# Two 16 KB activation tiles are placed ahead of the small constants in the on-chip memory, in a three-layer fp32 network on one core

## The chip, the cores and the metric

The kernel runs on 1 core of one Trainium2 chip. The metric is device time of one execution in microseconds (us), the median of several runs; lower is better. In names below, PE is TensorE, DVE is VectorE, ACT is ScalarE, POOL is GpSimd, SP is SyncE; PEld are the weight loads of PE. SBUF is the on-chip memory of 128 partitions in which all tiles lie; a tile's address is a byte within each partition.

## The reference

Three layers act on one sequence of 512 positions with 1024 features, all in float32. Cut to what matters:

```python
def hybrid_layer(x, ...):                      # twice
    u = rms_norm(x, g_mix_pre) @ w_in          # 1024 -> 3200
    aq, ak, av, cu, rq, rk, rv, rg = split(u)
    mix = concat([chunk_attention(aq, ak, av), conv_module(cu), retention(rq, rk, rv, rg)]) @ w_out
    x = x + rms_norm(mix, g_mix_post)
    f = square(relu(rms_norm(x, g_mlp_pre) @ w_up)) @ w_down      # 1024 -> 4096 -> 1024
    return x + rms_norm(f, g_mlp_post)

def second_block(x, ...):                      # once
    q, k, v, u, gates = split(rmsnorm(h, norm1_gain) @ w_in)      # 1024 -> 5632
    branches: difference attention on q, k, v; a state-space layer on u; sigmoid(gates)
    h = h + (g_attn * attn_branch + g_ssm * ssm_branch) @ w_out
    up = causal_dwconv(rmsnorm(h, norm2_gain) @ w_up)             # 1024 -> 5632
    gate, val = split(up)
    return h + (silu(gate) * val) @ w_down                        # 2816 -> 1024
```

## The kernel before

**Three matmuls for one.** Float32 products are made from the type float32r, in which one matmul pass does not keep all bits. Each operand is therefore split into a high part (a cast) and a low part (the rest), and each 128x128 block product takes three matmuls: high by high, high by low, low by high (`mm3`, L863, and `t_part`, L911). PE is given a stationary operand (128 columns, loaded beforehand) and a moving operand (up to 512 columns, streamed).

```python
nc.tensor.matmul(ps, whi, ahi, start=start, stop=False)     # out, stationary, moving
nc.tensor.matmul(ps, whi, alo, start=False, stop=False)
nc.tensor.matmul(ps, wlo, ahi, start=False, stop=stop)
```

**The tiles of the change.** `hhi` and `hlo` (L999, L1000) hold the high and low part of the normalised activations, transposed: 128 partitions of 8 x 512 floats, 16,384 bytes of a partition each. `to_hT` (L985) writes them, before each of the large products that start from the normalised x. They are read in two ways:

- In `f_unit` (L890) and `f_split` (L896) a chunk of weights (tiles `whi`, `wlo`) is stationary and `hhi`/`hlo` move, 512 columns at a time (256 in `f_split`). So are made w_up of all layers, most of the first layers' w_in, the gates, and the attention projection, for which the two tiles are filled anew. The same function, with other moving tiles (`ghi`, `glo`, `shi`, `slo`), makes w_glu and w_ssm_proj.
- In `t_unit` (L922) 128 columns of `hhi`/`hlo` are stationary and the weights move, 384 or 512 columns at a time: v, q and k of the layers. The same function makes w_down and w_out, with `fhi`/`flo`, `mixhi`/`mixlo` or `mhi`/`mlo` stationary.

A trace names a matmul `ps<-moving,stationary`, so `ps<-hhi,whi` is of the first kind and `ps<-whi,hhi` of the second.

**The rest of the work.** Weights stream from HBM through SP's queue in chunks of 128x1024 floats into 4 slots (`wraw`); ACT casts each into `whi`, DVE or POOL subtracts to make `wlo` (4 slots each). Attention, retention, convolution and the state-space layer run as side tasks on DVE, ACT and POOL between the matmuls.

**The order of the work.** The program is recorded first (`Builder.run`), then a planner (`Trace.order`, L443) sets the order of all instructions by its own costs and due times, and `issue` (L638) writes them out in that order. The planner looks at which slot of a pool a tile has, never at an address.

**Where a tile lies.** Tiles are lazy: the real one is made when the first instruction that uses it is written out (L324, L365). `hhi`, `hlo` and the constants come from the pool `cp` (`bufs` None), which gives each new tile the next free bytes, rounded up to 32.

```python
    def place(self):
        if self.real is None:
            self.real = self.pool.make(self)
        return self.real
```

So the order of first use sets the addresses. Before, this is `mhalf` (128 bytes, from byte 16512), `ones` (512), `epsc` (4), `cm` (2048), `pv` (3208), `hhi`, `rope` (1024), `hlo`, and some small ones. `hhi` starts at byte 22464 and `hlo` at byte 39872; both are 192 bytes past a multiple of 256. The slots of `wraw`, `whi` and `wlo` (from byte 61184, 4096 each) and the 55 slots of the pool `sp` (from byte 110336, 2048 each), in which every other large tile lies, start at multiples of 256. Any block of `hhi` or `hlo` that a matmul reads starts a multiple of 512 bytes into the tile.

Of the kernel before, what the change touches and what calls it, by code (L numbers as in the profile page):

```python
# [2060 lines left out]
@with_exitstack  # L2061
def hybrid_stack_kernel(ctx: ExitStack, tc, A, out):
    b = Builder(tc, ctx, A, out)
    b.run()
    order = b.nc.order()
    with tc.manual_schedule():
        b.nc.issue(order)

# [17 lines left out]
```

## Time and profile before

| what | value |
|---|---|
| median of 3 runs | 2149.17 us (2148.69 to 2149.26) |
| the profiled execution: its own time | 2147.38 us |
| its span, first to last instruction | 2145.7 us |
| PE busy | 2050.4 us, 96% of the span, 9964 matmuls |
| DVE / ACT / POOL busy | 64% / 43% / 34% |
| DMA | 105 GB/s mean |

A matmul's recorded length is longer than the distance to the next one, since matmuls overlap in the pipeline. This distance, from start to start, is called the pitch here. It is read from a timeline (starts of two matmuls, divided by the steps between them) or from a window in which PE never stops: in a window of 20 us with 90 matmuls, the first one began up to its own length of 0.39 us earlier, so the pitch is about (20 + 0.39) / 90 = 226.6 ns.

A row of the view by windows has, in this order: the window's start and end, its length, the busy time (and number of instructions) of PE, PEld, DVE, ACT and, where it worked, POOL, the granted share of PE's clock, the DMA engines' busy share and the GB/s they moved.

### The profile page before, as it was taken

How to read it: one execution, taken by the hardware profiler on the slowest of the kernel's cores; microseconds unless marked ns; L12 is line 12 of the kernel's file. 1: busy time of each engine (PE TensorE's matmuls, PEld its weight loads, DVE VectorE, ACT ScalarE, POOL GpSimd, SP SyncE). 2: the span in 40 equal slices, each digit the busy share in tenths (PEclk: the TensorE clock that was granted, in tenths of full speed). 3: DMA queues.
4: the chain of work that ended last, by engine and by line, in shares of the span. 5: the costliest groups of instructions: out<-in, count | busy, mean ns of one | idle time of the engine just before them, and what ended most of it. 6: DMA issues, size and time to landing. Idle time of an engine off the chain costs nothing. (4 is left out here: it accounts for less than half of the span.)

```text
span 2145.7 us, 27037 instructions
## 1 busy us (share of the span) xinstructions
PE 2050.4 (96%) x9964; PEld 1703.7 (79%) x9964; DVE 1365.4 (64%) x2127; ACT 931.5 (43%) x1527; POOL 726.4 (34%) x858
## 2 busy tenths in 40 slices
PE   7998989999999998899999999999999999999999
PEld 7987778778889977688888887677777788888887
DVE  5998795344458998553454473478889546655545
ACT  3377534222334376443233244456578234333322
POOL 3662367960005652300000036754653431000000
PEclk9999999999999999999999998999999999999999
DMA  5423333333243332223233363222324423233322
GB/s 180 128 61 126 109 104 128 109 108 98 79 125 96 121 96 92 95 83 99 79 105 102 89 205 117 90 84 74 97 75 157 157 79 109 89 99 98 99 79 79
DMA packets 85556, 225.16 MB, mean 105 GB/s; under 512 B 10416, under 2 KB 20400, under 8 KB 85424
## 3 DMA queue, kind: packets, MB, share of 16 engines
q1 hardware_dynamic: 85424, 223.43, 32.7%
q8 instruction: 79, 1.29, 0.3%
q14 instruction: 53, 0.43, 0.1%
HBM read 204.25 MB, written 19.14 MB: 104 GB/s over the span
## 5 line engine op out<-in xcount | busy, mean ns | idle before, releaser
L642 POOL TENSOR_TENSOR wlo<-wraw,whi 128x1024 fp32r<-128x1024 f32 (+1 forms) x156 | 365.8, 2353 | 1079.5 <-ACT whi L642 883.3
L642 ACT CAST whi<-wraw 128x1024 fp32r<-128x1024 f32 (+1 forms) x323 | 330.4, 1029 | 703.8 <-PE ps L642 567.2
L642 PE MATMUL ps<-hhi,whi 128*128 128x512 f32 (+1 forms) x1488 | 506.8, 370 | 7.5 <-DVE acc L642 1.9
L642 PE MATMUL ps<-hlo,whi 128*128 128x512 f32 (+1 forms) x1488 | 505.8, 369 | 6.9 <-DVE hlo L642 6.9
L642 PE MATMUL ps<-hhi,wlo 128*128 128x512 f32 (+1 forms) x1488 | 505.3, 369 | 0.5 <-DVE wlo L642 0.5
L642 PEld LDWEIGHTS ps<-hhi,whi 128*128 128x128 f32 x1488 | 273.0, 191 | 56.3 <-issue 4.1
L642 PEld LDWEIGHTS ps<-hlo,whi 128*128 128x128 f32 x1488 | 272.8, 191 | 54.6 <-DVE hlo L642 7.9
L642 PEld LDWEIGHTS ps<-hhi,wlo 128*128 128x128 f32 x1488 | 272.3, 191 | 48.9 <-DVE wlo L642 1.4
L642 DVE TENSOR_TENSOR wlo<-wraw,whi 128x1024 fp32r<-128x1024 f32 x178 | 223.9, 1259 | 114.7 <-ACT whi L642 114.2
L642 PE MATMUL ps<-whi,fhi 128*128 128x512 f32 x688 | 249.6, 392 | 4.8 <-DVE t L642 2.4
L642 PE MATMUL ps<-whi,flo 128*128 128x512 f32 x688 | 249.8, 391 | 0.0
L642 PE MATMUL ps<-wlo,fhi 128*128 128x512 f32 x688 | 249.7, 391 | 0.0
L642 DVE TENSOR_TENSOR acc<-ps,acc 128x512 f32<-128x512 f32 x112 | 76.5, 687 | 155.1 <-PE ps L642 155.1
L642 PE MATMUL ps<-wlo,hhi 128*128 128x384 f32 (+1 forms) x448 | 157.5, 371 | 3.9 <-POOL wlo L642 3.9
L642 PE MATMUL ps<-whi,hhi 128*128 128x384 f32 (+1 forms) x448 | 156.0, 372 | 0.9 <-ACT whi L642 0.7
L642 PEld LDWEIGHTS ps<-whi,fhi 128*128 128x128 f32 x688 | 129.5, 188 | 33.3 <-DVE t L642 2.9
L642 PE MATMUL ps<-whi,hlo 128*128 128x384 f32 (+1 forms) x448 | 155.2, 369 | 0.0
L642 PEld LDWEIGHTS ps<-whi,flo 128*128 128x128 f32 x688 | 129.7, 188 | 28.0
L642 PEld LDWEIGHTS ps<-wlo,fhi 128*128 128x128 f32 x688 | 129.7, 189 | 27.8
L642 POOL TENSOR_TENSOR st<-st,mhalf 128x1 f32<-128x1 f32 (+1 forms) x56 | 55.0, 983 | 194.9 <-DVE st L642 192.9
L642 DVE TENSOR_SCALAR t<-ps 128x512 f32<-128x512 f32 x64 | 44.1, 690 | 93.9 <-PE ps L642 93.8
L642 DVE TENSOR_TENSOR X<-ps,X 128x512 f32<-128x512 f32 x56 | 38.6, 689 | 92.3 <-PE ps L642 92.1
(249 smaller groups left out, 3250.2 us busy)
## 6 DMA issues: line engine op xcount, KB each, us to landing
wraw<-in_wst SPq DMA_DIRECT2D x302, 512.0 KB, 3.5
wraw<-in_wst SPq DMA_DIRECT2D x32, 384.0 KB, 3.1
gain<-in_gains SPq DMA_DIRECT2D x20, 256.0 KB, 4.3
X<-in_x SPq DMA_DIRECT2D x16, 256.0 KB, 5.4
xd<-X SPq DMA_DIRECT2D x16, 256.0 KB, 2.1
X<-xd SPq DMA_DIRECT2D x16, 256.0 KB, 5.6
gated<-t SPq DMA_DIRECT2D x16, 256.0 KB, 2.1
gate<-gated SPq DMA_DIRECT2D x16, 256.0 KB, 3.7
```

Source lines behind the costliest of these rows:

```text
L642: getattr(getattr(self.nc, e), m)(*[r(x) for x in op.args], **{k: r(v) for k, v in op.kw.items()})
```

## The change

Right after the planner has set the order, three tiles are made, before the first instruction is written out: `mhalf`, then `hhi` and `hlo`.

```diff
     b.run()
     order = b.nc.order()
+    for t in (b.mhalf, b.hhi, b.hlo):
+        t.place()
     with tc.manual_schedule():
         b.nc.issue(order)
```

`mhalf` is named first because it is 128 bytes long and the pool begins 128 bytes past a multiple of 256. `hhi` now starts at byte 16640 and `hlo` at byte 33024, both multiples of 256. `ones`, `epsc`, `cm`, `pv` and `rope` follow at 49408 to 56256 and keep their distance to the last multiple of 256 (0, 0, 32, 32 and 192 bytes). Every other tile keeps its address. No instruction is added, removed or changed but for these addresses, and on each of the five engines the instructions stand in the same order, row for row.

## Rows read from the trace of the kernel before

**Rows 1.** The page's head: span, and busy time by engine.

```profile
span 2145.7 us, 27037 instructions
PE 2050.4 (96%) x9964; PEld 1703.7 (79%) x9964; DVE 1365.4 (64%) x2127; ACT 931.5 (43%) x1527; POOL 726.4 (34%) x858
```

**Rows 2.** The chain of work that ended last: start, length, what.

```profile
1780.76 361.13 PE ps L642 x1640
```

**Rows 3.** Groups of PE's instructions by form: count, busy us, mean ns of one.

```profile
L642 PE MATMUL ps<-hhi,wlo 128*128 128x512 f32 x1104 | 420.1, 397 | 0.5 <-DVE wlo L642 0.5
L642 PE MATMUL ps<-whi,flo 128*128 128x512 f32 x688 | 249.8, 391 | 0.0
L642 PE MATMUL ps<-whi,hlo 128*128 128x384 f32 x256 | 79.1, 338 | 0.0
L642 PE MATMUL ps<-wlo,hhi 128*128 128x512 f32 x192 | 78.1, 413 | 0.0
L642 PE MATMUL ps<-klo,stk 128*128 128x512 f32 x40 | 16.4, 409 | 3.9 <-DVE klo L642 3.9
```

**Rows 4.** Windows without a stop: two of hhi/hlo moving, two of weights moving.

```profile
1800.00:1864.00 64.00, 64.00 (x276) 51.58 (x275) 39.23 (x48) 27.19 (x36) 2.40 (x1) 1.00 0.31 99
1687.00:1727.00 40.00, 40.00 (x173) 32.20 (x173) 29.37 (x21) 11.54 (x14) 18.70 (x8) 1.00 0.46 158
1739.00:1759.00 20.00, 20.00 (x90) 16.49 (x89) 2.77 (x4) 6.55 (x11) 9.47 (x4) 1.00 0.37 103
2118.00:2135.00 17.00, 17.00 (x77) 14.08 (x76) 7.88 (x10) 2.11 (x2) 0.00 (x0) 1.00 0.04 16
```

**Rows 5.** Timeline of PE where f_unit has shi and slo moving: start, length.

```profile
1666.23 0.50 PE L642 MATMUL ps<-slo,whi 128*128 128x512 f32 x1 [0.97 <-DVE slo L642]
...
1667.72 0.40 PE L642 MATMUL ps<-shi,whi 128*128 128x512 f32 x1
...
1669.10 0.62 PE L642 MATMUL ps<-shi,whi 128*128 128x512 f32 x2
...
1671.82 0.39 PE L642 MATMUL ps<-shi,whi 128*128 128x512 f32 x1
```

**Rows 6.** Timeline of PE with hhi and hlo stationary, weights moving.

```profile
84.04 0.34 PE L642 MATMUL ps<-whi,hhi 128*128 128x384 f32 x1
...
85.60 0.34 PE L642 MATMUL ps<-whi,hhi 128*128 128x384 f32 x1
...
1583.67 0.40 PE L642 MATMUL ps<-whi,hlo 128*128 128x512 f32 x1
...
1586.94 0.40 PE L642 MATMUL ps<-whi,hhi 128*128 128x512 f32 x1
```

**Rows 7.** Timeline of PE in f_split, 256 columns of hhi and hlo moving.

```profile
1774.69 0.28 PE L642 MATMUL ps<-hhi,whi 128*128 128x256 f32 x1
...
1775.03 0.28 PE L642 MATMUL ps<-hhi,whi 128*128 128x256 f32 x1
```

**Rows 8.** Windows, stretches where PE hardly stops.

```profile
500.00:600.00 100.00, 100.00 (x436) 81.53 (x435) 48.30 (x54) 31.74 (x39) 8.07 (x3) 1.00 0.36 106
350.00:450.00 100.00, 92.36 (x381) 73.27 (x380) 40.36 (x61) 27.49 (x34) 97.34 (x259) 0.96 0.35 116
935.00:1265.00 330.00, 330.00 (x1444) 269.68 (x1443) 156.15 (x194) 108.08 (x146) 18.89 (x12) 1.00 0.33 102
1680.00:1730.00 50.00, 50.00 (x217) 40.44 (x216) 32.94 (x24) 13.74 (x16) 21.41 (x10) 1.00 0.45 152
1798.00:2141.00 343.00, 343.00 (x1488) 279.04 (x1487) 188.96 (x229) 114.99 (x145) 12.06 (x5) 1.00 0.29 91
```

**Rows 9.** Windows, the stretches with side tasks.

```profile
0.00:300.00 300.00, 266.69 (x1509) 237.58 (x1510) 248.53 (x441) 159.87 (x301) 146.89 (x160) 0.98 0.35 114
650.00:935.00 285.00, 262.44 (x1512) 234.05 (x1511) 233.16 (x378) 151.86 (x290) 123.15 (x138) 0.99 0.30 96
1265.00:1680.00 415.00, 388.85 (x1923) 306.63 (x1922) 296.45 (x539) 244.49 (x440) 230.30 (x169) 0.98 0.35 110
```

## The prediction

> **What bounds the kernel now.** I read the page's head first [rows 1]: PE is busy 2050.4 of 2145.7 us, so only about 95 us of the span are not matmuls. The chain of waits says the same of the end: its last piece but one is 361 us of PE without a wait, 1640 matmuls one behind the other [rows 2]. So the time is, for the most part, the number of matmuls times their pitch, and the question is whether an address can change a pitch.
>
> The groups by form then show something odd [rows 3]. With 512 columns moving, `ps<-hhi,wlo` lasts 397 ns on average and `ps<-whi,flo` 391 ns. These means hold waits and a slower clock in places, so I went to windows without a stop, all at a granted clock of 1.00 [rows 4]. Where `hhi`/`hlo` move, 276 matmuls fill 64 us: (64 + 0.40) / 276 = **233.3 ns** each; the second such window gives (40 + 0.40) / 173 = 233.5. Where weights move and `mhi`/`mlo` are stationary, (20 + 0.39) / 90 = **226.6 ns**; the window near the end, with `fhi`/`flo`, gives 225.8. The shape and the type are the same in all four. Other engines hardly matter: the fourth window, with POOL idle, is as fast as the third, with POOL at work half of the time, and the first is slow with POOL as good as idle.
>
> The two kinds differ in who moves, so a control is needed. Rows 5 are it: the same function `f_unit`, weights stationary, but `shi`/`slo` moving, which lie in slots of `sp` at multiples of 256. From 1669.10 to 1671.82 there are 12 steps: 2.72 / 12 = 226.7 ns. So not the function and not the roles make 233; what is left is the tile, and the programmed difference of `hhi` and `hlo` is their start, 192 bytes past a multiple of 256. As stationary operand they seem to cost as well: from 1583.67 to 1586.94 are 14 steps of 233.6 ns with 512 columns of weights moving, and from 84.04 to 85.60 nine steps of 173.3 ns with 384 columns [rows 6]; three quarters of 226.7 would be 170.0.
>
> **The change part by part.** No instruction is added, removed or reordered, so no queue is passed and no wait is new. `ones`, `epsc`, `cm`, `pv` and `rope` move, but keep their distance to a multiple of 256: I cost them at nothing, between no gain and no loss. ACT's and DVE's writes of the two tiles I cost at nothing too: they lie beside PE's work in all but a few places. What can change is the pitch of every matmul that reads `hhi` or `hlo`. I take 227.0 ns for what it becomes with 512 columns, a little over the 226.7 of a settled run, because a run takes some matmuls to settle (after the wait at 1666.23 the six steps from 1667.72 to 1669.10 are still 230 ns each [rows 5]).
>
> *Stretches where PE never stops* [rows 8]. Here f_unit and t_unit alternate, and the mean pitch lies between the two values. What each gives if it falls to 227.0:
>
> - 1798 to 2141: (343 + 0.39) / 1488 = 230.8; 1488 x 3.8 ns = 5.7 us.
> - 935 to 1265: (330 + 0.39) / 1444 = 228.8; 1444 x 1.8 ns = 2.6 us.
> - 500 to 600: (100 + 0.39) / 436 = 230.3; 436 x 3.3 ns = 1.4 us. The same pattern runs from 450 on and from 300 to 350: twice this, 2.8 us.
> - 1680 to 1730: (50 + 0.39) / 217 = 232.2; 217 x 5.2 ns = 1.1 us.
>
> Together **12.2 us**. All of it is on the path: DVE is busy 189 of 343 us and 156 of 330, POOL hardly at all, so the preparation of weights keeps up with a PE that is 1.5% quicker.
>
> *350 to 450.* POOL is busy 97.34 of 100 us and PE waits. 381 matmuls x 3.3 ns would be 1.3 us; a quicker PE waits longer for POOL here, so I take 0.3 us, with 0 and 1.3 as bounds.
>
> *Stretches with side tasks* [rows 9]. Of the 3312 matmuls with 512 moving columns of `hhi`/`hlo`, 9 chunks x 24 in each of two layers and 16 gates x 24, 816 in all, lie here: 816 x 6.3 ns (233.3 less 227.0) = 5.1 us. 576 have them stationary at 512 columns (3 x 192 [rows 3]); with the 233.6 of rows 6 as a ceiling, I take half of 6.6 ns: 1.9 us. 768 have them stationary at 384 columns: 3.3 ns x 768 = 2.5 us. Together 9.5 us. With 256 columns moving I expect nothing: 1774.69 to 1775.03 are three steps of 113.3 ns [rows 7], exactly half of 226.7. How much of the 9.5 reaches the end? PE is busy 918 of these 1000 us; in the rest it waits, and DVE is busy 778 us. A quicker PE arrives earlier at the same wait. I take half, **4.7 us**, with 0 and 9.5 as bounds.
>
> Sum: 12.2 + 0.3 + 4.7 = 17.2 us. The profiled execution took 2147.4 us and lies 1.8 us under the median of the runs shown, 2149.2. So the changed profile should read about 2130.2 and the median **2132.0 us**, 0.8% less. With every bound at its best, 23.0 us, it is 2126; since transfers and preparation shift with it, I allow 3 us beyond. With the bounds at their worst, 12.2 us, it is 2137.
>
> One rule of the Trainium skill speaks against all of this. Both the old and the new starts are multiples of 64 bytes. The page "SBUF — State Buffer", section "Specifications (TRN2)", counts in cachelines of 16 bytes, and says nothing of larger ones. By it a contiguous read from either start crosses as many lines, and the sum would be 0, the second rival below. The trace does not agree so far: 233.3 against 226.6 in contiguous reads of one size.
>
> **The rivals.**
>
> *Half of it.* In the mixed stretches the pitch of 230 may come in part from the alternation itself, since each switch of roles disturbs a settled run as a wait does; and in the side-task stretches DVE may take back everything. Then half of 12.2 is left: 6 us, 2143. For it: runs need time to settle [rows 5]. Against it: the slow pitch is at its full height where nothing alternates [rows 4].
>
> *No effect.* The 233 ns belong to something else in these tiles (their place below the weights, their row length), not to the start. For it: at 256 columns the same tiles show no loss [rows 7], though they start just as oddly, and `ps<-klo,stk` lasts 409 ns with both operands at multiples of 256 [rows 3]. Against it: those are short runs between waits, which never settle, and the control of rows 5. Price: 0, 2149.
>
> *Slower: equal starts collide.* PE reads the moving operand and the next stationary one at the same time. With `hhi` at 192 and `whi` at 0 they may now be kept apart, and with both at 0 meet. `ps<-klo,stk`, both at 0, is the row for it: 409 ns, 12 ns more than `ps<-hhi,wlo`. If all 3312 went there, 40 us: 2189. It decides where the moving group's length in a window without stops rises over its present 396 to 397 instead of falling to 389 to 391. Against it: `shi` with `whi`, both at 0, ran at 226.7 [rows 5].
>
> **How the numbers follow.** About 0.2%, 4.3 us, is what a measurement of this kernel tells from no change. The forecast has 0.68, all of it faster. Half of it has 0.19, of which 0.17 faster by more than 0.2%. No effect has 0.09 and the collision 0.04. So faster 0.85, same 0.11, slower 0.04. The range goes from 2123, the best bound, to 2143, which takes in the forecast's worst bound and most of the half case, some 0.8.
>
> **What would show it.** Right: the window of the first large f_unit run of the last stretch (now 1800 to 1864) reads 226 to 227 ns; all `hhi`/`hlo` groups at 512 columns drop towards 391 ns; those at 256 stay; PE's busy time falls by 15 to 25 us with the same 9964 matmuls; waits for DVE grow by some us. Wrong: a pitch of 233 at the new address (no effect), 230 in mixed stretches only (half), over 233 (collision). The terms are off if the last stretch, now 343 us for 1488 matmuls, shrinks by much other than 5.7 us.

## The result, and the profile after

The changed kernel takes **2134.83 us** (median of 5 runs, 2132.77 to 2137.03), the kernel before 2148.69 us in 5 runs beside them. The ratio is 0.9932, with a 95% interval of 0.9922 to 0.9943: 0.68% or 14 us faster. The forecast was 2132.0, so 3 us of the expected 17 are missing.

The profiled execution of the changed kernel took 2135.72 us. Its page's head, which answers [rows 1]:

```profile
span 2134.0 us, 27037 instructions
...
PE 2036.2 (95%) x9964; PEld 1709.2 (80%) x9964; DVE 1362.7 (64%) x2127; ACT 931.8 (44%) x1527; POOL 727.8 (34%) x858
```

The same 9964 matmuls keep PE busy 14.2 us less, and the span is 11.7 us shorter than that of the profiled execution before. The chain of waits, whose PE piece answers [rows 2]:

```profile
1774.57 355.66 PE ps L642 x1640
```

These 1640 matmuls without a wait, the same in both, take 5.47 us less. PE's groups by form, which answer [rows 3], with the three forms of `f_split` added:

```profile
L642 PE MATMUL ps<-hhi,wlo 128*128 128x512 f32 x1104 | 414.9, 392 | 0.4 <-DVE wlo L642 0.3
L642 PE MATMUL ps<-whi,flo 128*128 128x512 f32 x688 | 249.3, 390 | 0.0
L642 PE MATMUL ps<-hhi,whi 128*128 128x256 f32 x384 | 88.7, 295 | 2.8 <-ACT hhi L642 1.9 <-DVE x L642 1.0
L642 PE MATMUL ps<-hlo,whi 128*128 128x256 f32 x384 | 87.9, 295 | 6.8 <-DVE hlo L642 6.8
L642 PE MATMUL ps<-hhi,wlo 128*128 128x256 f32 x384 | 87.1, 291 | 0.0
L642 PE MATMUL ps<-whi,hlo 128*128 128x384 f32 x256 | 79.5, 339 | 0.0
L642 PE MATMUL ps<-wlo,hhi 128*128 128x512 f32 x192 | 77.8, 412 | 0.0
```

`ps<-hhi,wlo` at 512 columns fell from 397 to 392 ns and now stands beside `ps<-whi,flo`. The forms at 384 columns did not fall (338 before, 339 now), and those at 256 columns *rose*, from 293, 291 and 288 ns to 295, 295 and 291. The windows show this as pitches; the first three answer [rows 4], the fourth lies in `f_split`, the rest answer [rows 8] and [rows 9], in part:

```profile
1794.00:1857.00 63.00, 63.00 (x280) 52.16 (x279) 39.93 (x49) 27.87 (x37) 2.40 (x1) 1.00 0.32 101
1682.00:1721.00 39.00, 39.00 (x173) 32.30 (x173) 25.50 (x22) 12.17 (x15) 20.94 (x8) 1.00 0.48 162
1733.00:1753.00 20.00, 20.00 (x89) 16.51 (x89) 2.77 (x4) 6.74 (x12) 9.48 (x4) 1.00 0.33 105
1777.00:1792.00 15.00, 15.00 (x127) 15.00 (x126) 5.99 (x8) 5.70 (x7) 2.40 (x1) 1.00 0.13 38
500.00:600.00 100.00, 100.00 (x443) 82.81 (x442) 49.96 (x56) 33.30 (x42) 7.99 (x3) 1.00 0.35 106
350.00:450.00 100.00, 91.01 (x383) 73.10 (x381) 40.83 (x61) 27.43 (x34) 97.26 (x263) 0.97 0.35 116
1798.00:2134.00 336.00, 332.22 (x1466) 274.86 (x1464) 185.32 (x224) 111.28 (x139) 10.06 (x5) 1.00 0.29 93
0.00:300.00 300.00, 266.41 (x1488) 237.81 (x1489) 246.26 (x439) 158.72 (x300) 144.84 (x159) 0.98 0.35 114
650.00:935.00 285.00, 262.33 (x1506) 234.70 (x1507) 232.49 (x377) 151.07 (x288) 122.56 (x138) 0.99 0.30 95
1265.00:1680.00 415.00, 389.18 (x1928) 309.07 (x1926) 293.54 (x536) 240.14 (x432) 227.74 (x168) 0.99 0.35 110
```

- `hhi`/`hlo` moving, 512 columns: (63 + 0.39) / 280 = 226.4 ns, where 233.3 stood. By the starts of its 285 matmuls this run is settled at 226.67.
- Mixed stretches: (100 + 0.39) / 443 = 226.6 ns for 230.3, and (332.22 + 0.39) / 1466 = 226.9 for 230.8.
- 256 columns: (15 + 0.28) / 127 = **120.3 ns**, where [rows 7] had 113.3. PEld is busy for the whole window here, but for only 52 of 63 us in the first one.
- Side tasks: the first 300 us hold 1488 matmuls, 21 *fewer* than before, and 650 to 935 holds 6 fewer. The same windows hold somewhat shifted work, so the table further down compares the same matmuls.

The timeline, which answers [rows 6] and [rows 7]:

```profile
83.82 0.33 PE L642 MATMUL ps<-whi,hhi 128*128 128x384 f32 x1
...
86.94 0.33 PE L642 MATMUL ps<-wlo,hhi 128*128 128x384 f32 x1
...
1581.26 0.39 PE L642 MATMUL ps<-whi,hhi 128*128 128x512 f32 x1
...
1584.88 0.39 PE L642 MATMUL ps<-wlo,hhi 128*128 128x512 f32 x1
...
1769.21 0.40 PE L642 MATMUL ps<-hhi,wlo 128*128 128x256 f32 x2
...
1770.17 0.40 PE L642 MATMUL ps<-hhi,whi 128*128 128x256 f32 x2
```

With 384 columns of weights moving, 18 steps take 3.12 us: 173.3 ns, as before. With 512 moving over `hhi`/`hlo`, 16 steps from 1581.26 to 1584.88 are 226.3 ns (233.6 before). In `f_split`, eight steps from 1769.21 to 1770.17 are exactly 120.0.

Where the difference came from can be added up from the starts of the matmuls in the two traces. For each step from one start to the next I take what it is longer than 0.4427 ns per column (226.67 ns for 512), and sum this over the steps that are less than 9% longer, which leaves out waits:

| matmuls | before, us | after, us | difference |
|---|---|---|---|
| 512 columns, `hhi`/`hlo` moving | 19.0 | 2.5 | -16.5 |
| 512 columns, weights moving over other tiles | 3.3 | 0.8 | -2.5 |
| 512 columns, `hhi`/`hlo` stationary | 1.9 | 1.3 | -0.6 |
| 384 columns, `hhi`/`hlo` stationary | 2.6 | 3.1 | +0.5 |
| 256 columns, `hhi`/`hlo` moving | 1.6 | 6.3 | +4.7 |

The sum is -14.4 us. Steps longer than that, waits above all, grew by 2.9 us over all 9964 matmuls, and the other short steps lost 0.2. Together this is the 11.7 us between the two spans. The waits vary from one execution to the next: in two more traces of the changed kernel they grew by 3.6 and by 0.4 us, and the span fell by 11.1 and 14.2.

Both traces have the 9964 matmuls in the same order. So the time from one matmul to another can be compared, stretch by stretch (named by the times before):

| stretch | forecast, us | measured, us | of it 512 / 384 / 256 columns / waits |
|---|---|---|---|
| where PE hardly stops: 300 to 350, 450 to 650, 935 to 1265, 1680 to the end | -12.2 | -14.4 | -15.3 / 0 / +1.1 / -0.2 |
| 350 to 450 | -0.3 | 0.0 | -1.3 / 0 / 0 / +1.4 |
| with side tasks: 0 to 300, 650 to 935, 1265 to 1680 | -4.7 | **+2.7** | -3.1 / +0.5 / +3.7 / +1.8 |

All of the gain lies where PE hardly stops. The stretches with side tasks became longer; in the two more traces of the changed kernel they did so by 3.5 and by 1.9 us.

### The profile page after: what moved, and what is told of

It is laid out like the page before. It is cut to its first block, busy times and chain, and to the rows that moved or that the text cites. A ratio compares the mean times of both kernels' runs of the same rounds, so it can differ in the third digit from the quotient of the medians.

```text
span 2134.0 us, 27037 instructions
## 1 busy us (share of the span) xinstructions
PE 2036.2 (95%) x9964; PEld 1709.2 (80%) x9964; DVE 1362.7 (64%) x2127; ACT 931.8 (44%) x1527; POOL 727.8 (34%) x858
```

## The experiments

**The question.** The forecast explained 233 against 227 ns by the start of `hhi` and `hlo`. That explanation (A: the start itself, modulo 256) left the 256 columns without a reason, and the change moved the tiles lower in memory as well (C: the place). The rival B: what counts is the *distance*, the start of the moving block minus the start of the stationary one, modulo 256 bytes. All experiments start from the changed kernel, and move tiles by padding, or write a chunk of weights further on in its slot; the order of the instructions stays. In the results below, settled pitches are means over the longest runs of one kind, by the starts in the trace; a settled run repeats a short pattern of steps (at 233.3 ns before the change, 231 and 236 in turn).

**Everything at 192.** 48 floats of padding shift `hhi`, `hlo`, all weight slots and all of `sp` together.

```diff
-    for t in (b.mhalf, b.hhi, b.hlo):
+    p0 = b.cp.tile(F32, "pada", [P, 48])
+    for t in (b.mhalf, p0, b.hhi, b.hlo):
```

> As the changed kernel, but 192 bytes are left free after mhalf, so that hhi, hlo, the weight slots and all slots of sp start 192 bytes past a multiple of 256: every distance between a moving and a stationary tile is as in the changed kernel, every start is as odd as hhi's was before. Theory A (what counts is the start itself against multiples of 256): now all 512-column runs are slow, 233 ns in the f_unit run near 1800 us and 233 ns or more also in the w_down runs that read 226.6 before; time over 2149 us, some 2165. Theory B (what counts is the distance between the moving and the stationary tile, modulo 256): 226.7 ns everywhere with 512 columns, 120 ns with 256, time as the changed kernel, 2133 to 2137. Theory C (the place ahead of the constants, lower in the memory, not the start): 226.7 ns for hhi, time as the changed kernel.

Measured: 2136.51 us, ratio to before 0.9947 (0.9932 to 0.9962). Two windows of it, one of `f_unit` and one of `f_split`:

```profile
1795.00:1859.00 64.00, 64.00 (x284) 52.98 (x283) 40.94 (x50) 28.18 (x37) 2.40 (x1) 1.00 0.31 100
1778.00:1793.00 15.00, 15.00 (x128) 15.00 (x127) 6.07 (x8) 6.02 (x8) 2.41 (x1) 1.00 0.12 36
```

(64 + 0.39) / 284 = 226.7 ns and (15 + 0.28) / 128 = 119.4: the pitches of the changed kernel, at the starts, modulo 256, that `hhi` and `hlo` had before. A falls.

**The two tiles at other distances.** `hlo` alone at 192, then both tiles at 128, then both at 64, all else at 0. The edit of the second (the others differ in the sizes and the place of the padding):

```diff
-    for t in (b.mhalf, b.hhi, b.hlo):
+    p0, p1 = b.cp.tile(F32, "pada", [P, 32]), b.cp.tile(F32, "padb", [P, 32])
+    for t in (b.mhalf, p0, b.hhi, b.hlo, p1):
```

> As the changed kernel, but hlo alone is put back to 192 bytes past a multiple of 256; hhi stays at a multiple. If each matmul pays for its own moving tile: in a long f_unit run the hlo third at 233, the others at 226.7, mean 228.9, and half to two thirds of the gain stays: 2138 to 2141 us. If one odd tile of three is enough to keep the run from settling: 231 to 233 throughout, about 2146. If only hhi matters: as the changed kernel, 2133 to 2137. With 256 columns: between 113 and 120 ns, since the changed kernel has 120 and the kernel before 113.

> As the changed kernel, with hhi and hlo 128 bytes past a multiple of 256 and all other large tiles at multiples of 256. Theory A with 256 as the unit: 233 ns with 512 columns, 113 with 256, time as before, 2146 to 2150. With 128 as the unit: 226.7 and 120 ns, time as the changed kernel. A start that is good for both, 226.7 with 512 columns and 113 with 256, would give about 2129. Theory C (place): 226.7 ns whatever the start.

> As the changed kernel, with hhi and hlo 64 bytes past a multiple of 256. Theory A: 233 ns with 512 columns, 113 with 256, 2146 to 2150 us. If the phase between the two read streams counts and not a crossing of lines, 64 and 192 may differ: anything between 226.7 and 236 ns. Theory C (place): 226.7 ns.

Measured: `hlo` alone 2146.52 us, ratio 0.9996 (0.9987 to 1.0006); both at 128 2150.73 us, 1.0016 (1.0006 to 1.0026); both at 64 2144.47 us, 0.9984 (0.9975 to 0.9993). The long `f_unit` runs in the trace of each, first with `hlo` alone off, then with both at 128:

```profile
1799.00:1864.00 65.00, 65.00 (x282) 52.74 (x281) 40.74 (x50) 28.17 (x37) 2.42 (x1) 1.00 0.32 100
1690.00:1730.00 40.00, 40.00 (x173) 32.20 (x172) 29.33 (x21) 11.39 (x14) 18.85 (x8) 1.00 0.45 158
```

With both at 64, and a window in `f_split`:

```profile
1798.00:1862.00 64.00, 64.00 (x281) 52.52 (x280) 40.38 (x49) 28.20 (x37) 2.41 (x1) 1.00 0.32 101
1781.50:1796.50 15.00, 15.00 (x130) 15.00 (x129) 6.11 (x8) 5.97 (x8) 2.41 (x1) 1.00 0.13 38
```

These are (65 + 0.40) / 282 = 231.9 ns, (40 + 0.40) / 173 = 233.5, (64 + 0.39) / 281 = 229.1 and (15 + 0.28) / 130 = 117.5. With `hlo` alone off, this run wandered between 225 and 240 ns and did not settle (mean 231.4), though two thirds of its matmuls have `hhi` moving; three other long runs had the same mean, and three settled at 228.9. That 228.9 is also what one third of 233.3 and two thirds of 226.7 give, but no matmul pays for its own tile alone: over all runs the steps with `hhi` moving, at distance 0, are 229.8 and 230.1 ns (227.5 in the changed kernel), those with `hlo` 231.4. One operand at another distance disturbs the whole run. In all three the tiles lie low in memory, and the gain is gone or mostly gone. So C falls too.

**The weights at 192 as well, `sp` at 0.** A gap of 64 bytes is put between the weight slots and `sp`.

```diff
+        self.gp = pool("gp", None)
         self.sp = pool("sp", ...
...
+    p0, p1 = b.cp.tile(F32, "pada", [P, 48]), b.gp.tile(F32, "padb", [P, 16])
+    for t in (b.mhalf, p0, b.hhi, b.hlo, p1):
```

> hhi, hlo and the weight slots start at 192 modulo 256, all of sp (fhi, flo, shi, slo and the others) at 0. The distance theory (the pitch follows the moving start minus the stationary start, modulo 256, in bytes) expects: 512 columns with hhi or hlo moving over weight tiles, distance 0, 226.7 ns settled; weight tiles moving over fhi or flo in the down and out projections and shi or slo moving over weight tiles, distances 192 and 64, no longer the 226.7 ns of the changed kernel but 233.3 and 228.9 ns; 256 columns with hhi moving 120.0 ns as in the changed kernel. Time: 512 columns with weight tiles and sp tiles paired are about 1,400 matmuls, so 3 to 9 us above the changed kernel, 2138 to 2144 us. The rival, that only the start of hhi and hlo against the other tiles of the kernel decides (every start in its own right), expects the sp pairs to stay at 226.7 ns, since neither fhi nor shi has moved, and 2134 to 2137 us.

Measured: 2151.83 us in one run (before 2148.43). Windows of it: `f_unit` with `hhi`/`hlo`, then two in which weights move over tiles of `sp`:

```profile
1806.00:1870.00 64.00, 64.00 (x284) 53.02 (x283) 40.94 (x50) 28.08 (x37) 2.40 (x1) 1.00 0.34 100
604.00:641.00 37.00, 37.00 (x160) 29.87 (x159) 18.79 (x26) 10.43 (x19) 1.10 (x2) 1.00 0.37 123
1226.00:1263.00 37.00, 37.00 (x160) 29.89 (x159) 21.29 (x40) 10.99 (x21) 1.10 (x2) 1.00 0.37 116
```

The first pair keeps 226.7 ns. The other two stand at (37 + 0.40) / 160 = 233.7, where the changed kernel has 226.7, although `fhi` and `flo` still start at multiples of 256; and `shi`/`slo` moving over weights (distance 64) went to 229.0. All three as B has it. The time was 8 us over my range: I had counted some 1400 matmuls for these pairs, and there are 2639 of weights moving over other tiles alone, 16 us by their mean pitch of 233.0.

**A distance that is no multiple of 64.** Both tiles at 32, with 8 and 56 floats of padding in place of 32 and 32 above.

> hhi and hlo start at 32 modulo 256, everything else at 0: a distance that no run has had, and no multiple of 64. If the pitch goes by steps of 64 bytes, the settled 512-column pitch with hhi moving is that of distance 0 (226.7 ns) or of 64 (228.9 ns), about 2135 to 2145 us; if a start off a multiple of 64 costs something of its own, it is above 233.3 ns, and the time above 2149 us; if the pitch goes evenly with the distance it is about 227.8 ns and the 256 columns about 118.9 ns, near 2140 us.

Measured: 2150.25 us in one run, 512 columns settled at 233.3 ns, 256 columns at 116.7 (two of thirteen stretches near 117.8). Windows of it, 512 and 256 columns:

```profile
1802.00:1867.00 65.00, 65.00 (x280) 52.24 (x279) 40.24 (x49) 27.48 (x36) 2.41 (x1) 1.00 0.31 98
1785.00:1799.00 14.00, 14.00 (x122) 14.00 (x121) 5.55 (x8) 5.74 (x7) 2.41 (x1) 1.00 0.14 39
```

None of the three cases that I had named: 233.3 is the pitch of 192, not above it, not that of 0 or 64, and not between.

**The best of both.** The 24 chunks that `f_split` takes are written 64 bytes further on in their slots, which are made 256 bytes longer. Then only the 256-column pairs have distance 192.

```diff
+    SPLIT = {i + j for i in (0, 37, 101, 138, 202, 268) for j in range(4)}
...
-            hi = self.b.wh.tile(name="whi")
-            lo = self.b.wl.tile(name="wlo")
+            o = 16 if j in self.SPLIT else 0
+            hi = self.b.wh.tile(name="whi")[:, o:o + 1024]
+            lo = self.b.wl.tile(name="wlo")[:, o:o + 1024]
...
-        self.wh, self.wl = pool("wh", self.NW, [P, 1024], F32R), pool("wl", self.NW, [P, 1024], F32R)
+        self.wh, self.wl = pool("wh", self.NW, [P, 1088], F32R), pool("wl", self.NW, [P, 1088], F32R)
```

> The changed kernel, but the 24 weight chunks that f_split takes (256 columns, 1152 matmuls) lie 64 bytes further on in their slots, so that hhi and hlo moving over them have the distance 192 as before the change, and every 512-column pair keeps distance 0. The distance theory expects 256 columns at 113.3 ns settled instead of 120.0, 512 columns still at 226.7 ns; by the mean pitches (114.9 ns before, 119.55 after, 1152 matmuls) about 5 us less than the changed kernel, up to 7.7: 2127 to 2130 us. The rival, that the 256-column matmuls became slower because the tiles lie lower in memory or because the 512-column work around them is faster, expects 120.0 ns and 2134 to 2136 us.

> The changed kernel once more, unaltered, beside the run before it on the same chip: 2133 to 2137 us, 256 columns at 120.0 ns, 512 columns at 226.7 ns.

Measured: 2133.66 us (0.993, 0.9917 to 0.9943) beside 2135.71 us for the unaltered changed kernel (0.994, 0.9926 to 0.9953). Windows of the first: `f_unit`, then two stretches of `f_split`:

```profile
1790.00:1853.00 63.00, 63.00 (x280) 52.13 (x279) 39.95 (x49) 27.86 (x37) 2.41 (x1) 1.00 0.31 101
1773.00:1788.00 15.00, 15.00 (x129) 15.00 (x129) 6.11 (x8) 5.99 (x8) 2.41 (x1) 1.00 0.11 37
919.00:929.00 10.00, 10.00 (x90) 10.00 (x89) 5.91 (x8) 4.64 (x8) 0.00 (x0) 1.00 0.18 54
```

512 columns stay at 226.4, although the longer slots lie in turn at odd and even multiples of 256: for them the period is 256 bytes and not 512. No stretch of 256 columns is at 120.0 any more, but they settle in two ways: the second window gives (15 + 0.28) / 129 = 118.4 ns, the third 10.28 / 90 = 114.2. By the starts, 7 of the 13 long stretches are at 117.8 and 6 at 113.3. The mean falls from 119.5 to 115.9, 3.7 us less in all, not the 5 to 7.7 expected. The kernel before had both ways too, which the forecast had missed; a window of its trace:

```profile
658.00:663.50 5.50, 5.50 (x49) 5.50 (x48) 5.06 (x10) 2.68 (x8) 1.58 (x2) 1.00 0.68 202
```

5.78 / 49 = 118.0 ns: 3 of its 13 stretches are like this.

The two were run once more side by side, since the times of five runs each overlap:

> The kernel with f_split's chunks 64 bytes further on, once more, beside the changed kernel on the same chip, to settle a difference that five runs each left open (2133.66 against 2135.71, ranges overlapping). By the trace the 256-column steps are 3.7 us shorter in it (mean pitch 115.9 against 119.55 ns, 1152 matmuls). If that reaches the end: 2 to 4 us below the changed kernel, 2130 to 2134 us. If it is taken back by waits: the same as the changed kernel within 1 us.

> The changed kernel, unaltered, for the comparison with the run beside it: 2133 to 2137 us.

Measured: 2132.30 us (2129.51 to 2134.17) beside 2133.93 us (2132.93 to 2137.99). Over the ten runs of each the means are 2132.9 and 2135.3 us; the difference of 2.3 us has a standard error of 0.9. So this version is probably the fastest of all, by 0.1%; the steps show its gain more sharply than the times do. In this second trace 4 of the 13 stretches are at 117.8 and 9 at 113.3: three that had 117.8 in the first execution now have 113.3, so which way a stretch settles is not fixed by the program.

**Two more distances for 256 columns.** The same with 32 bytes and with 96 bytes in place of 64.

> As the run with f_split's chunks 64 bytes further on in their slots, but 32 bytes: the distance of hhi and hlo from these weights is 224 modulo 256, which no run has had. In the run with 64 bytes seven of the thirteen long stretches of 256 columns settled at 117.8 ns and six at 113.3 (two each way in the kernel before: 2 to 3 of thirteen at 117.8). The distance theory has no value for 224; it expects anything but the 120.0 ns of distance 0, and 226.7 ns at 512 columns. If every distance but 0 has two settled patterns, both appear here too; time 2130 to 2135 us. If instead only the chunks' being off their slots' start matters, it is as with 64 bytes, 113.3 and 117.8 ns in the same stretches.

> The same with 96 bytes, distance 160. The run with hhi and hlo at 128 gave 118.6 ns at distance 128, the ones at 192 and 64 gave 113.3 and 117.8: between 128 and 192 the distance theory expects 113 to 119 ns at 256 columns and 226.7 ns at 512; time 2130 to 2136 us. A value of 120.0 ns would say that multiples of 256 are not the only distance with the long pitch.

Measured, one run each: 2135.42 and 2134.29 us. A window of the first, and one of the second:

```profile
1777.00:1791.50 14.50, 14.50 (x125) 14.50 (x124) 5.92 (x8) 5.68 (x7) 2.40 (x1) 1.00 0.10 37
920.50:931.50 11.00, 11.00 (x94) 11.00 (x93) 6.46 (x8) 5.12 (x7) 0.00 (x0) 1.00 0.16 49
```

These are 14.78 / 125 = 118.2 and 11.28 / 94 = 120.0 ns. At distance 224 all 13 stretches are at 118.3 to 118.8, at 160 they are at 117.3, at 118.6 to 118.8, and one at 120.0. So two settled values are no rule for every distance, and 120.0 is not reserved to distance 0; 192 has the lowest one.

The settled pitches in ns, by distance (moving start minus stationary start, modulo 256):

| distance | 512 columns | 256 columns |
|---|---|---|
| 0 (changed kernel, all at 192) | 226.7 | 120.0 |
| 32 | 233.3 | 116.7, seldom 117.8 |
| 64 | 228.9 (in the kernel before, with weights moving, also 233.5) | 117.8, once 113.3 |
| 128 | 232.4 to 233.3 | 118.7 |
| 160 | not tried | 117.3, 118.7, 120.0 |
| 192 (before; the weights at 192 with `sp` at 0) | 233.3 | 113.3, 117.8 |
| 224 (for 512: weights moving over `hhi`/`hlo` at 32) | 233.3 | 118.3 |

## Why the prediction was right, and where it was not

**The forecast, at its core: right.** It said that an address sets the pitch of 512-column matmuls, and that 233.3 becomes 226.7; it became 226.67. The shift of everything by 192 bytes shows that the reason was half right. It is not the start at a multiple of 256 that helps, but the agreement with the other operand: the forecast's control, `shi` over weights [rows 5], was fast because both lay at 0, and the change worked because the weight slots and `sp` lie there. That a rule about the start alone gave the right new start is luck: with the weights at 192, `fhi` and `flo` at multiples of 256 were in the slow place (233.7 ns). The time, too, came closer than its terms: by the table of stretches one gave 2.2 us more than forecast and another 7.4 us less.

**Stretches where PE never stops, 12.2 us: right, somewhat low; 350 to 450, 0.3 us: nothing came.** By the sums of steps at 512 columns, the stretches 300 to 650, 935 to 1265 and from 1680 on gave 16.6 us. They fell to 226.67 without the 0.33 ns that I allowed for settling (0.33 ns x 4,717 steps = 1.6 us), and 600 to 650 was not in my sum. From 935 to 1265 the term had 2.6 us and 4.5 came: 14 of its 1444 matmuls have 128 or 256 columns, and these short ones pulled the mean of 228.8 down. The last 1488 matmuls gained 6.3 us, where the term had 5.7. From 350 to 450 the steps became 1.3 us shorter and PE's waits 1.4 us longer, so this stretch took as long as before, the lower bound of its term; the waits that grew there end with DVE's `acc` (4.3 to 5.6 us), and that POOL holds them up is not shown. The rival "half of it" is gone with this. The 230 ns of mixed stretches came for the most part from the slow pairs (16.5 us). The other pairs gained 2.5 us too: before, all but 0.1 of their 3.3 us lay in the first 15 steps after a change of pair, where after it 0.7 is left.

**Side tasks, 4.7 us: wrong, they became 2.7 us longer, outside the bounds of 0 and 9.5.** 7.0 us at 512 columns, halved to 3.5, stands against 3.1 measured for all 512-column steps of these stretches; but the halving was for waits, and the steps themselves gave less than half. For 384 columns the term had 2.5 us (halved, 1.25), because three quarters of 226.7 is 170.0. The pitch stayed at 173.3 to 173.7, and the sum rose by 0.5 us. The scaling by columns had no row behind it, and the rows of 256 columns were already a sign against it. What turned the term round are 3.7 us of the 256 columns (the next paragraph) and 1.8 us of longer waits.

**256 columns, "I expect nothing": the step that failed.** 113.3 is half of 226.7, and I took it for a pitch that has nothing to lose or gain; under the rivals I even set these rows aside as short runs that never settle, though one of them has 130 steps at 113.3. It was the best case of distance 192, and distance 0 costs 120.0: +4.7 us over 1152 matmuls, more than the 3 us by which the forecast was short. Here, and only here, equal starts were the slower ones, as the rival "equal starts collide" had it; whether two reads collide no run shows. I had priced it on 512 columns alone. The sign "those at 256 stay" failed with this, and PE's busy time fell by 14.2 us, just short of the 15 to 25. The version with `f_split`'s chunks at another distance took 3.7 us of steps and 2.3 us of time back (standard error 0.9), so that this loss is shown and not only argued.

**Waits.** I expected half of the side-task gain to be taken back by waits for DVE. Those for `t` did not grow (19.6 us, 19.8 before). All steps with waits grew by 2.9 us, 1.4 of it from 350 to 450 and 1.8 in the side-task stretches.

**The rules.** "SBUF — State Buffer" of the Trainium skill, section "Specifications (TRN2)", counts in cachelines of 16 bytes, by which the forecast had a sum of 0. The traces do not agree: distances that are all multiples of 32 bytes differ by up to 6.7 ns. The page "TensorE: Matmul & The Clock Gate" of the Trainium skill, section "Step-by-step: what each phase is for", says that loading the next weights takes no read bandwidth from the running matmul, as each has its own port. By that alone one would expect no effect of the distance between the two, and the traces show one, 226.7 to 233.3 ns; that it is bandwidth of a port that they share is not shown.

**What stays open.** Why an equal start helps at 512 columns and hurts at 256. A sign is that PEld is busy in the whole of a 256-column window, but in 52 of 63 us at 512, so that the load may be what sets the pitch there; but it is so at 114 ns as well as at 120. No run here separates the load's reads from the moving operand's.

## What to carry to other kernels

Read the pitch of long runs without a stop, pair by pair, before trusting that one shape has one speed: 3% of a matmul's pitch stood in the addresses here, 0.7% of the kernel's time, and three tiles made earlier brought it back. What to bring into agreement is the moving and the stationary operand of a matmul with 512 columns, modulo 256 bytes; for fewer columns measure first, because at 256 the same agreement cost 6% of a settled run and 4% in the mean. A shorter pitch also gives nothing where PE waits anyway: from 350 to 450, 1.3 us of shorter steps came back as waits. When a control is taken from a trace, list everything in which it agrees with the good case: here both operands lay at 0, and the forecast credited one.

## What was not expected of the hardware

- The pitch goes by the distance of the two operands modulo 256 bytes and is not even in it: 226.7, 233.3, 228.9 ns at 0, 32 and 64 bytes.
- At 256 columns, one distance (192) settles at 113.3 or at 117.8 ns, in the same program on the same stretch: the stretch from about 292 us was at 117.8 in one execution and at 113.3 in another.
- One of the operands at another distance affects the steps of the others: with `hlo` alone off, steps of 225 to 240 ns all through 65 us, and 229.8 ns and more on average where `hhi` moves at distance 0.
